# A hybrid DeltaNet and attention layer: the last stage in two phases with the output product as seven block products, and the attention merge moved beside the inverse and the scan

## The chip, the cores and the metric

One core of a Trainium2 chip runs the whole layer as one program. The metric is the time of one execution in device microseconds; the median of three runs is given. The engines are named as in the profile: PE is TensorE (PEld its weight loads), DVE VectorE, ACT ScalarE, POOL GpSimd, SP the engine that issues the DMA transfers. Each executes its own instructions in order; semaphores order them between engines.

## The reference

x has 2048 tokens of 1024 channels in float32. One input projection feeds two token mixers of four heads of 128 channels: a gated DeltaNet in chunks of 64, whose unit lower-triangular matrices are inverted, and a dilated window attention in three groups, whose outputs are merged by their softmax denominators. Cut to what matters here:

```python
tmat = lax.linalg.triangular_solve(eye + lower, eye, left_side=True, lower=True, unit_diagonal=True)
...
xs = tuple(jnp.moveaxis(a, 2, 0) for a in (q, k, u, w, a_intra, gc))
_, o = lax.scan(step, s0, xs)
...
alpha = jax.nn.softmax(jnp.stack(lses, axis=0), axis=0)
o_swa = jnp.sum(alpha[..., None] * jnp.stack(outs, axis=0), axis=0)
o_dn = rms_norm(o_dn, dn_norm_w) * jax.nn.silu(dn_z);  y_dn = o_dn @ w_branch_dn
o_swa = o_swa * jax.nn.silu(swa_z);  y_swa = o_swa @ w_branch_swa
merged = jax.nn.sigmoid(g_dn) * y_dn + jax.nn.sigmoid(g_swa) * y_swa
x = x + merged @ w_out
```

The two branch products are 2048 x 512 by 512 x 1024 each, the output product 2048 x 1024 by 1024 x 1024.

## The kernel before, in words

Every product is made in three passes: each operand is split into a high part (`split`: ACT rounds to fp32r, L87) and the rest (a subtraction on DVE or POOL, L88), and high by high, high by low and low by high are summed in PSUM.

The work comes in this order, as PE sees it: the input projection of the attention part with the attention itself beside it (to some 1000 us); the projections of the DeltaNet part, of z and of the gates (`cunits`, L720 to L722, 24 matmuls 128x512 for each chunk of 128 columns and 512 tokens; three PSUM tiles `mm`); from 1976 us the last stage. Beside the projections' matmuls runs a list of events: every six matmuls `hook` counts one tick, and what `at(delay, ...)` put down for that tick is issued there. Where a pool or the scheduler leaves an instruction free, its place on its engine may still differ from the place in the code.

Beside the projections run, in turn: the inverse of the 128 triangular matrices on DVE (`inverse`, 63 rows, each a product L1020 and a reduction L1023; M is stored to `vscr`, its transposed copy Z, made half by ACT in L1014 and half by DVE in L1015, to `tscr`); the scan over 16 tiles of 128 tokens (`scan`, its loads of `rec`, `t` from `tscr` and `vb` from `vscr` at L1042 to L1048, its first matmul L1058); in the last chunks, the tail, the loads and splits of the final weights (`w_fin`, `w_split`), and the first attention merges. The gate chunks end in a tanh on ACT (L1155) and a store to `gscr`; their weights are split by L87 and L88.

`combine(t)` (L1187 to L1207) merges the three attention groups of a tile of 128 tokens: it loads `oc` (3 groups, 4 heads, 128 channels and two statistics, 780 KB) and does a dozen operations on DVE and one exponential on ACT. `o_prep` transposes a tile of a branch on PE (L1221), gates it with z on DVE (L1222) and splits it.

The last stage goes through eight blocks of 256 tokens. `fin_y` makes, for each of eight groups of 128 output channels, both branch products (L1237 to L1239, 24 matmuls 128x256), gates them on DVE (L1241), adds them on POOL (L1243) and splits the sum (L1244, L1245) into mh and ml. `fin_out` then multiplies mh and ml by w_out, four times 24 matmuls 128x512 (L1254 to L1256), adds x on DVE (L1260) and stores the result. So the output product of a block follows its branches at once, and the merges, loads and weight splits of later blocks run beside it.

## Time and profile before

| | us |
|---|---|
| median of 3 runs | 2356.08 (2354.23 to 2360.46) |
| the profiled execution | 2357.82 |
| its span, first to last instruction | 2356.0 |
| its mean granted TensorE clock | 0.99 |

The page gives busy time by engine, a chain of work followed back from the last instruction, and groups of instructions with the idle time before them. A row of the timeline has the start in the span, the duration, the engine, the line, the operation and its tiles, and in brackets the idle time of the engine before it and what ended it. Matmuls overlap, so their spacing, not their duration, is what one costs.

### The profile page before, as it was taken

The numbers are of one execution on the slowest core, as the hardware profiler recorded it, in microseconds if no ns is written. First come the engines' busy times: TensorE is split into PE (matmuls) and PEld (weight loads), VectorE is DVE, ScalarE is ACT, GpSimd is POOL, SyncE is SP. The second block draws the span as 40 slices with busy tenths as digits, with TensorE's granted clock in tenths as the row PEclk, the third lists the DMA queues.
The fourth block names the chain that finished last, engine by engine and source line by source line (L and its number), as shares of the span: only waits on it lengthen the run. The fifth ranks groups of instructions, "written<-read, shape, count | busy, mean of one in ns | idle before, by whom it ended". The sixth has DMA issues, their size and how long they took to land.

```text
span 2356.0 us, 43344 instructions
## 1 busy us (share of the span) xinstructions
PE 2297.1 (97%) x15216; PEld 2086.2 (89%) x15216; DVE 1347.7 (57%) x2853; ACT 907.2 (39%) x2948; POOL 889.2 (38%) x1331
## 2 busy tenths in 40 slices
...
GB/s 296 325 277 323 272 283 292 269 161 239 251 265 236 246 273 261 259 148 101 130 110 132 127 103 113 72 76 69 212 207 208 193 120 175 161 179 150 148 139 77
DMA packets 525969, 452.23 MB, mean 192 GB/s; under 512 B 66168, under 2 KB 490424, under 8 KB 523320
## 3 DMA queue, kind: packets, MB, share of 16 engines
...
q14 instruction: 96, 0.79, 0.1%
...
## 4 chain that ended last, share of the span: by engine, by line
PE 66%; DMA 5%; DVE 3%; POOL 1%; ACT 1%; issue 1%; SPq 0%; DVEq 0%; POOLq 0%; ACTq 0%
PE mm L433 12%; PE mm L720 10%; PE mm L721 10%; PE mm L722 10%; PE mm L1254 2%; PE mm L1256 2%; PE mm L1255 2%; PE mm L1237 2%; PE mm L1239 2%; PE mm L1238 2%; DMA oscr<-ol 2%; DMA gcb<-gcscr 1%; PE tp L584 1%; PE po L626 1%; DMA raw<-in_w_out_dram 1%; PE tp L617 1%
## 5 line engine op out<-in xcount | busy, mean ns | idle before, releaser
L720 PE MATMUL mm<-hh,w 128*128 128x512 f32 x1152 | 463.3, 402 | 0.0
L722 PE MATMUL mm<-hh,w 128*128 128x512 f32 x1152 | 457.8, 397 | 0.0
L721 PE MATMUL mm<-hl,w 128*128 128x512 f32 x1152 | 456.9, 397 | 0.0
L433 PE MATMUL mm<-w,hh 128*128 128x256 f32 x1760 | 328.3, 286 | 0.0
L433 PEld LDWEIGHTS mm<-w,hh 128*128 128x128 f32 x1760 | 271.2, 190 | 0.0
L88 POOL TENSOR_TENSOR w<-raw,w 128x512 fp32r<-128x512 f32 x68 | 100.0, 1472 | 435.0 <-ACT w L87 434.8
L720 PEld LDWEIGHTS mm<-hh,w 128*128 128x128 f32 x1152 | 220.3, 191 | 45.9
L722 PEld LDWEIGHTS mm<-hh,w 128*128 128x128 f32 x1152 | 217.0, 188 | 46.9
L433 PE MATMUL mm<-hh 128*128 128x256 f32 x880 | 257.5, 293 | 0.0
L721 PEld LDWEIGHTS mm<-hl,w 128*128 128x128 f32 x1152 | 217.6, 189 | 42.4
L433 PE MATMUL mm<-hl,hh 128*128 128x256 f32 x880 | 249.8, 284 | 0.9 <-POOL hl L295 0.9
L433 PE MATMUL mm<-hh,hl 128*128 128x256 f32 x880 | 249.6, 284 | 0.0
L433 PE MATMUL mm<-w,hl 128*128 128x256 f32 x880 | 248.3, 282 | 0.0
L607 DVE CUSTOM_DVE_ANT_0 p<-sc,mask 128x128 f32<-128x128 f32 (+1 forms) x192 | 70.0, 365 | 213.8 <-PE sc L604 87.0
L433 PEld LDWEIGHTS mm<-hl,hh 128*128 128x128 f32 x880 | 169.4, 192 | 1.3 <-POOL hl L295 1.3
L433 PEld LDWEIGHTS mm<-hh 128*128 128x128 f32 x880 | 169.3, 192 | 0.0
L433 PEld LDWEIGHTS mm<-hh,hl 128*128 128x128 f32 x880 | 169.0, 192 | 0.0
L433 PEld LDWEIGHTS mm<-w,hl 128*128 128x128 f32 x880 | 166.1, 189 | 0.0
L368 POOL TENSOR_SCALAR st<-st 128x4 f32<-128x4 f32 x96 | 21.1, 219 | 374.0 <-ACT junk L367 371.9
L1237 PE MATMUL mm<-oh,hh 128*128 128x256 f32 x512 | 143.7, 281 | 1.7 <-DVE gt L1241 1.7
L1239 PE MATMUL mm<-oh,hl 128*128 128x256 f32 x512 | 142.9, 279 | 0.0
L1238 PE MATMUL mm<-ol,hh 128*128 128x256 f32 x512 | 142.9, 279 | 0.0
...
## 6 DMA issues: line engine op xcount, KB each, us to landing
...
qks<-rec SPq DMA_DIRECT2D x96, 256.0 KB, 3.2
raw<-in_w_in_dram SPq DMA_DIRECT2D x68, 256.0 KB, 3.3
gscr<-gt SPq DMA_DIRECT2D x64, 256.0 KB, 2.5
gt<-gscr SPq DMA_DIRECT2D x64, 256.0 KB, 3.4
...
```

What stands on the lines that cost most here:

```text
L88: eng.tensor_tensor(out=l, in0=raw, in1=h.bitcast(F32), op=ALU.subtract)
L433: mm = lambda x, y, **kw: nc.tensor.matmul(o, x, y, skip_group_check=True, **kw)
L607: nc.vector.tensor_tensor_reduce(out=p[:, lo:hi], in0=sc[:, lo:hi], in1=self.mask[:, slot * P + lo:slot * P + hi], scalar=3e38, scale=-SCA ...
L720: nc.tensor.matmul(pr, wh[:, k, :], a, start=(k == 0), stop=False)
L721: nc.tensor.matmul(pr, wh[:, k, :], b, start=False, stop=False)
L722: nc.tensor.matmul(pr, wl[:, k, :], a, start=False, stop=(k == KT - 1))
L1237: nc.tensor.matmul(o, self.wbh[:, k, ms], oh[:, k, :], start=(k == b * 4), stop=False)
L1238: nc.tensor.matmul(o, self.wbh[:, k, ms], ol[:, k, :], start=False, stop=False)
L1239: nc.tensor.matmul(o, self.wbl[:, k, ms], oh[:, k, :], start=False, stop=(k == b * 4 + 3))
L1254: nc.tensor.matmul(pr, mh[:, k, cs], self.woh[:, k, hs], start=(k == 0), stop=False)
L1255: nc.tensor.matmul(pr, mh[:, k, cs], self.wol[:, k, hs], start=False, stop=False)
L1256: nc.tensor.matmul(pr, ml[:, k, cs], self.woh[:, k, hs], start=False, stop=(k == KT - 1))
```

## The change

Four things are changed.

1. `inverse` makes both halves of the transposed copy on DVE (L1018 of the changed kernel).
2. `combine` no longer runs in the tail and the last stage. One tile is merged every 15 ticks from the start of the inverse on, sixteen in all: the minimum on DVE (L1253), the exponential and the weighting of the groups (twelve operations 128x128, L1266) on ACT, all else on POOL (L1254 to L1262, the additions L1270); the tile is parked in DRAM, in `osd` (L1272), and `o_load` fetches it for `o_prep`. Tiles `oc` have two buffers. While the inverse runs, ACT and POOL keep the order of the code (`manual_schedule`).
3. The last stage does all eight blocks' branch products first. The merged sum goes to DRAM, to `mscr`; w_branch is laid out by output channel; the operands for w_out (four quarters and sums of them, `wo_chunk`) are made in blocks 0, 2, 4 and 5, two of them parked in DRAM and fetched in block 7.
4. Then the output product is made in eight groups of 256 tokens, each as seven block products of half size (the scheme of Strassen and Winograd, `PROD`), twelve matmuls 128x512 each. `m_op` prepares operands of tokens four products ahead; the partial results are added up in PSUM, on DVE and on POOL. z's factors 0.5 become 0.25, and the output's factor goes.

The order of DVE at the end of the inverse, before (L1020, L1023: a row of the inverse; L1015 its half of the copy; L1061 and L1084: the scan):

```order
L1023 TENSOR_REDUCE M<-Z 128x62
L1022 MEMSET M 128x1
L1020 TENSOR_TENSOR Z<-M 128x3969
L1021 MEMSET M 128x64
L1023 TENSOR_REDUCE M<-Z 128x63
L1022 MEMSET M 128x1
L1015 COPY Z<-M 128x2048
L1061 TENSOR_TENSOR zs<-sc,nbr 64x256
```

and in the changed kernel, where these lines are L1023, L1026 and L1018, and L1253 is the minimum in `combine` for tiles 12, 13 and 14:

```order
L1026 TENSOR_REDUCE M<-Z 128x62
L1025 MEMSET M 128x1
L1253 TENSOR_REDUCE cs<-oc 128x4
L1023 TENSOR_TENSOR Z<-M 128x3969
L1253 TENSOR_REDUCE cs<-oc 128x4
L1024 MEMSET M 128x64
L1026 TENSOR_REDUCE M<-Z 128x63
L1025 MEMSET M 128x1
L1018 COPY Z<-M 128x2048 x2
L1253 TENSOR_REDUCE cs<-oc 128x4
L1064 TENSOR_TENSOR zs<-sc,nbr 64x256
L1087 SCALAR_TENSOR_TENSOR rr<-sc,ksn,rec 128x128 x4
```

Three reductions that read a loaded tile `oc` have come between the last rows of the inverse, its copies and the scan.

SP's order at the same place, before (the stores of the inverse, L1012 and L1016, among loads of weights and stores of gates):

```order
L1156 DMA gscr<-gt 128x512
L697 DMA raw<-in_w_in_dram 128x4x128
L1156 DMA gscr<-gt 128x512
L1012 DMA vscr<-M 128x4096
L1016 DMA tscr<-Z 128x4096
L1156 DMA gscr<-gt 128x512 x2
L697 DMA raw<-in_w_in_dram 128x4x128
L1042 DMA rec<-rec 128x4x256
L1043 DMA rec<-rec 128x4x384
L1044 DMA lo_20483<-rec 64x4x64
L1046 DMA t_20487<-tscr 64x4x64
```

and after (L1272 parks a merged tile, L1241 loads the three groups of one, L1015 and L1019 are the stores of the inverse):

```order
L1159 DMA gscr<-gt 128x512
L1272 DMA osd<-oc 512x1x128
L1241 DMA oc<-oscr 128x1560
L1015 DMA vscr<-M 128x4096
L1019 DMA tscr<-Z 128x4096
L1159 DMA gscr<-gt 128x512 x2
L700 DMA raw<-in_w_in_dram 128x4x128
L1045 DMA rec<-rec 128x4x256
L1046 DMA rec<-rec 128x4x384
L1047 DMA lo_20785<-rec 64x4x64
L1049 DMA t_20789<-tscr 64x4x64
```

The two stores of the inverse now stand behind the parking of tile 12 and the load of tile 14.

DVE's order in the tail, before (L1222 gates a transposed tile, L1194 to L1206 merge the groups):

```order
L1194 TENSOR_REDUCE cs<-oc 128x4
L1195 TENSOR_TENSOR cs<-cs,oc 128x12
L1197 TENSOR_TENSOR cs<-cs,oc 128x12
L1198 TENSOR_REDUCE cs<-cs 128x4
L1222 SCALAR_TENSOR_TENSOR z<-tp,z 128x512
L1199 RECIPROCAL cs<-cs 128x4
L1200 TENSOR_TENSOR cs<-cs 128x12
L1203 TENSOR_TENSOR oc<-oc,cs 128x4x128 x3
L1205 TENSOR_TENSOR osw<-oc 128x512
L1206 TENSOR_TENSOR osw<-osw,oc 128x512
L1222 SCALAR_TENSOR_TENSOR z<-tp,dnw,z 128x512
```

and after (L1304 gates, L91 splits the branch weights):

```order
L1168 TENSOR_SCALAR dnw<-dnw 128x1
L1304 SCALAR_TENSOR_TENSOR z<-tp,dnw,z 128x512
L1304 SCALAR_TENSOR_TENSOR z<-tp,z 128x512
L1304 SCALAR_TENSOR_TENSOR z<-tp,dnw,z 128x512
L1304 SCALAR_TENSOR_TENSOR z<-tp,z 128x512
L91 TENSOR_TENSOR hl<-raw,hh 128x512
```

Nothing of the merge is left there. On PE nothing changes up to the end of the scan; in the last stage the 96 output matmuls of a block (L1254 to L1256) are gone from between the branch products, and 84 (L1411) for each group follow behind all of them.

The diff, cut to its core:

```diff
-                nc.scalar.activation(zt[:, 0:32, :], M.rearrange("p c i -> p i c")[:, 0:32, :], AF.Copy)
-                V.tensor_copy(zt[:, 32:64, :], M.rearrange("p c i -> p i c")[:, 32:64, :])
+                for r in (slice(0, 32), slice(32, 64)):
+                    V.tensor_copy(zt[:, r, :], M.rearrange("p c i -> p i c")[:, r, :])
...
+        self.W = {n: tuple(a[:, s, 4 * h:4 * h + 4, :] for a in (self.hh, self.hl))
+                  for n, (s, h) in (("B11", (2, 0)), ("B21", (2, 1)), ("T3", (3, 0)), ("B22", (3, 1)),
+                                    ("T1", (0, 0)), ("T4", (0, 1)))}
...
+    def wo_chunk(self, c):
+        nc, V = self.nc, self.nc.vector
+        cs = slice(c * P, (c + 1) * P)
+        r = {}
+        for n in FN:
+            r[n] = self.rawp.tile([P, 4, P], F32, name="raw") if n[2] == "1" else self.fp.tile([P, 4, P], F32, name="raw2", bufs=3)
+            off = (int(n[1]) - 1) * 512 * D + (int(n[2]) - 1) * 512 + c * P
+            nc.sync.dma_start(r[n], dr(self.i["w_out"], off, [[D, P], [P * D, 4], [1, P]]))
...
+        def first():
+            put("B11", r["B11"], V)
+            put("B22", r["B22"], nc.gpsimd)
+
+        def second():
+            sub(r["B11"], r["B12"], r["B11"])
+            t2 = r["T2"] = self.fp.tile([P, 4, P], F32, name="raw2", bufs=3)
+            sub(t2, r["B22"], r["B11"])
+            sub(r["B12"], r["B22"], r["B12"])
+
+        def fourth():
+            put("B21", r["B21"], V)
+            put("T3", r["B12"], nc.gpsimd)
+
+        def fifth():
+            sub(r["B21"], r["B21"], r["T2"])
+            put("T2", r["T2"], V)
+        for d, fn in ((6, first), (8, second), (10, lambda: park("T1", r["B11"], V)), (12, fourth), (14, fifth),
+                      (16, lambda: park("T4", r["B21"], nc.gpsimd))):
+            self.at(d, fn)
...
+    def comb_load(self, t):
+        oc = self.oc = self.cb.tile([P, G, H, 130], F32, name="oc", bufs=2)
+        self.nc.sync.dma_start(oc.rearrange("p g h c -> p (g h c)"),
+                               dr(self.oscr, t * P * G * H * 130, [[G * H * 130, P], [1, G * H * 130]]))
...
     def combine(self, t):
+        nc, cb, V = self.nc, self.cb, self.nc.gpsimd
+        oc = self.oc
+        if t < 15:
+            self.comb_load(t + 1)
+        sm = cb.tile([P, 4, 12], F32, name="cs", bufs=2)
         nm, ls = oc[:, :, :, 128], oc[:, :, :, 129]
         mn, e, c, r = sm[:, 0, 0:4], sm[:, 1, :].rearrange("p (g h) -> p g h", h=H), \
             sm[:, 2, :].rearrange("p (g h) -> p g h", h=H), sm[:, 3, 0:4]
+        nc.vector.tensor_reduce(out=mn.unsqueeze(2), in_=nm.rearrange("p g h -> p h g"), axis=mybir.AxisListType.X, op=ALU.min)
         V.tensor_tensor(out=e, in0=mn.unsqueeze(1).to_broadcast([P, G, H]), in1=nm, op=ALU.subtract)
+
+        def share():
+            nc.scalar.activation(e, e, AF.Exp)
+            V.tensor_tensor(out=c, in0=e, in1=ls, op=ALU.mult)
+            V.tensor_tensor(out=r, in0=c[:, 0], in1=c[:, 1], op=ALU.add)
+            V.tensor_tensor(out=r, in0=r, in1=c[:, 2], op=ALU.add)
+            V.tensor_tensor(out=r, in0=r, in1=self.mone, op=ALU.pow)
+            V.tensor_tensor(out=c, in0=e, in1=r.unsqueeze(1).to_broadcast([P, G, H]), op=ALU.mult)
+
+        def weigh(g):
+            for h in range(H):
+                nc.scalar.activation(oc[:, g, h, 0:P], oc[:, g, h, 0:P], AF.Identity, scale=c[:, g, h:h + 1])
+
+        def add(g):
+            o = oc[:, 0, :, 0:P]
+            V.tensor_tensor(out=o, in0=o, in1=oc[:, g, :, 0:P], op=ALU.add)
+            if g == 2:
+                nc.sync.dma_start(dr(self.osd, t * P * 512, [[512, P], [P, H], [1, P]]), o)
+        self.at(1, share)
         for g in range(G):
+            self.at(3 + g, lambda g=g: weigh(g))
+        for g in (1, 2):
+            self.at(4 + g, lambda g=g: add(g))
+        if t < 15:
+            self.at(15, lambda: self.combine(t + 1))
...
+    def o_plan(self, nb, d):
+        self.z = getattr(self, "z", {})
+        for j, (t, b) in enumerate(((2 * nb, 0), (2 * nb, 1), (2 * nb + 1, 0), (2 * nb + 1, 1))):
+            self.at(max(1, d + 3 * j - 4), lambda t=t, b=b: self.z_load(t, b))
+            self.at(d + 3 * j, lambda t=t, b=b: self.o_prep(t, b))
+            if b and nb < 7:
+                self.at(d + 3 * j + 1, lambda t=t: self.o_load(t + 2))
...
+    def fin_y(self, nb, m):
+        nc = self.nc
+        self.g_load(8 * nb + m + 2)
+        gt = self.gt.pop(8 * nb + m)
         pr = self.ps.tile([P, 512], F32, name="mm", bufs=3)
         for b in range(2):
             o = pr[:, b * 256:(b + 1) * 256]
+            oh, ol = self.o_tiles(nb, b)
+            for k in range(4):
+                wh, wl = self.wbh[:, m, 4 * b + k, :], self.wbl[:, m, 4 * b + k, :]
+                nc.tensor.matmul(o, wh, oh[:, k, :], start=(k == 0), stop=False)
+                nc.tensor.matmul(o, wh, ol[:, k, :], start=False, stop=False)
+                nc.tensor.matmul(o, wl, oh[:, k, :], start=False, stop=(k == 3))
             self.hook()
         nc.vector.scalar_tensor_tensor(out=gt, in0=gt, scalar=1.0, in1=pr.rearrange("p (b c) -> p b c", c=256),
                                        op0=ALU.add, op1=ALU.mult)
         nc.gpsimd.tensor_tensor(out=gt[:, 0, :], in0=gt[:, 0, :], in1=gt[:, 1, :], op=ALU.add)
+        nc.sync.dma_start(dr(self.mscr, nb * P * 2048 + m * 256, [[2048, P], [1, 256]]), gt[:, 0, :])
...
+        self.split(part[name] if name in part else ss[name], *self.m_slot(q), V if name in part else nc.gpsimd)
+        if i == 0:
+            new("S1", part["A21"], part["A22"], ALU.add)
+            new("S2", ss["S1"], part["A11"], ALU.subtract)
+            if g:
+                self.m_load(g + 1)
+        elif i == 2:
+            new("S3", part["A11"], part["A21"], ALU.subtract)
+        elif i == 4:
+            new("S4", part["A12"], ss["S2"], ALU.subtract)
...
+        for i, (_, tgt, first, wn) in enumerate(PROD):
+            q = 7 * g + i
+            self.at(1, lambda q=q: self.m_op(q + 4))
+            if first:
+                acc[tgt] = self.ps.tile([P, 512], F32, name="mm", bufs=3)
+            pr = acc[tgt]
+            ah, al = self.m_slot(q)
+            wh, wl = self.W[wn]
+            for k in range(4):
+                mm = lambda x, y, **kw: nc.tensor.matmul(pr, x, y, **kw)
+                mm(ah[:, k, :], wh[:, k, :], start=first and k == 0, stop=False, skip_group_check=True)
+                mm(ah[:, k, :], wl[:, k, :], start=False, stop=False, skip_group_check=True)
+                mm(al[:, k, :], wh[:, k, :], start=False, stop=(k == 3), skip_group_check=True)
+                if k % 2:
+                    self.hook()
+            if i == 0:
+                keep("p1", pr)
+            elif i == 1:
+                keep("u2", pr, hold["p1"])
+                plus("u2", 0, 1)
+            elif i == 2:
+                result(0, 0, pr, xo.pop((0, 0)))
+            elif i == 3:
+                keep("u3", pr, hold["p1"])
+                plus("u3", 1, 1)
+                plus("p1", 1, 0)
+            elif i == 4:
+                result(1, 1, pr, hold["u3"])
+            elif i == 5:
+                result(1, 0, pr, hold["p1"])
+            else:
+                result(0, 1, pr, hold["u2"])
...
+            ipin.enter_context(tc.manual_schedule(engines={E.Activation, E.Pool}))
             dst.close()
+            self.comb_setup(pool(bst, "cb"))
             self.inverse(pool(ist, "ip", "right"), start_scan)
...
+            ipin.close()
             ist.close()
             self.scan(pool(qst, "qp", "right"), start_fin)
...
+            self.o_load(0)
+            self.o_load(1)
+            self.o_plan(0, 8)
...
+        for nb in range(8):
+            if nb < 7:
+                self.o_plan(nb + 1, 4)
+            if nb in (0, 2, 4, 5):
+                self.wo_chunk((0, 2, 4, 5).index(nb))
+            if nb == 6:
+                self.at(8, lambda: self.m_load(0))
             for m in range(8):
-                self.fin_y(nb, m, oh, ol, mh, ml)
-                take((3, 3, 3, 3, 2, 2, 0, 0)[m])
-            if nb + 1 < nbk:
-                oh, ol = self.o_start(nb + 1, xo, 0 if nb else 6)
-            for t in (2 * nb, 2 * nb + 1):
-                for half in range(2):
-                    take(8)
-                    self.fin_out(t, half, mh, ml)
-            self.flush()
+                self.fin_y(nb, m)
+                if nb == 7 and m in (1, 3):
+                    self.fetch("T1" if m == 1 else "T4")
+                if nb == 7 and m < 4:
+                    self.at(3, lambda m=m: self.m_op(m))
...
+        self.p2 = pool(p2st, "p2", "right")
+        self.m_load(1)
+        for g in range(8):
+            self.group(g)
```

208 lines of the change are left out of this document (112 added, 96 removed).

## The prediction

> **What bounds the kernel now.** First the head of the page, the busy line and the chain that ended last:
>
> ```profile
> span 2356.0 us, 43344 instructions
> PE 2297.1 (97%) x15216; PEld 2086.2 (89%) x15216; DVE 1347.7 (57%) x2853; ACT 907.2 (39%) x2948; POOL 889.2 (38%) x1331
> PE 66%; DMA 5%; DVE 3%; POOL 1%; ACT 1%; issue 1%; SPq 0%; DVEq 0%; POOLq 0%; ACTq 0%
> ```
>
> TensorE is the bound, so a matmul that goes is worth its full spacing, and an edit elsewhere is worth only what PE stands still for it. Next the busy time by stretch, one of 128x512 matmuls alone and one of 128x256 alone:
>
> ```profile
> 1440.00:1640.00 200.00, 200.00 (x867) 163.72 (x866) 193.61 (x243) 31.95 (x54) 31.54 (x18) 1.00 0.23 73
> 1976.00:1990.00 14.00, 14.00 (x120) 13.96 (x119) 8.56 (x12) 7.57 (x14) 6.73 (x7) 1.00 0.85 233
> ```
>
> The columns after the stretch and its length are PE, PEld, DVE, ACT and POOL busy with their counts, then the granted clock, the DMA share and GB/s. 200/867 = 0.2307 us for a 128x512 matmul, 14/120 = 0.1167 us for a 128x256 one. Last, what PE waited for in the second half of the run:
>
> ```profile
> PE tp L1221 <- DVE osw L1206: 3.9, 1, 3.9
> PE mm L1254 <- ACT mh L1244: 2.2, 3, 1.0
> PE mm L1237 <- DVE gt L1241: 1.7, 2, 1.4
> ```
>
> Little is to be had from waits, then: 8 us, and what follows them.
>
> **The matmuls.** Before, the last stage has 8 token blocks of 192 matmuls 128x256 and 96 of 128x512: 1536 x 0.1167 + 768 x 0.2307 = 356.4 us of the some 380 that the stage takes (1976 to 2356). After, the first phase has the same 1536, and the second 8 groups of 7 products of 12, that is 672 of 128x512. 96 are gone: 96 x 0.2307 = **-22.1 us**. Nothing else on PE changes in number; up to the end of the scan its order is the same.
>
> **The merge of the attention groups** leaves the tail of the projections. There the trace has its one long wait:
>
> ```profile
> 1877.05 0.17 DVE L1194 TENSOR_REDUCE cs<-oc 128x4 f32<-128x12 f32 x1 [3.39 <-DMA oc<-oscr]
> 1879.09 4.05 DVE L1203 TENSOR_TENSOR oc<-oc,cs 128x512 f32<-128x512 f32 x3
> 1880.30 0.40 PE L722 MATMUL mm<-hh,w 128*128 128x512 f32 x1
> 1884.62 1.09 PE L1221 MATMUL tp<-ident,osw 128*128 128x128 f32 x4 [3.91 <-DVE osw L1206]
> 1886.36 0.63 PE L722 MATMUL mm<-hh,w 128*128 128x512 f32 x1
> 1886.78 0.63 PE L720 MATMUL mm<-hh,w 128*128 128x512 f32 x1
> 1881.00:1889.00 8.00, 4.38 (x13) 3.64 (x14) 4.96 (x7) 2.15 (x4) 4.73 (x4) 0.62 0.84 256
> ```
>
> The load of the three groups' tile lands late, DVE merges for 7 us, and PE waits 3.9. Then the granted clock is 0.62 over 8 us, and matmuls come 0.42 apart instead of 0.23: a loss of 8 x 0.38 = 3.0. After the change only a load of the merged tile stands there, issued with that of the DeltaNet tile that PE takes first, and what is late next is that transpose's z tile; I expect no wait. **-7 us** (-4 if a z tile is late).
>
> **The first block of the last stage.** Its weights are still being split while it runs:
>
> ```profile
> 1990.00:2000.00 10.00, 8.29 (x66) 7.68 (x65) 5.31 (x8) 3.66 (x7) 5.38 (x6) 1.00 0.79 217
> 2000.00:2007.00 7.00, 6.13 (x31) 4.42 (x29) 0.86 (x2) 1.57 (x4) 4.87 (x6) 1.00 0.30 94
> 2007.00:2012.00 5.00, 3.51 (x8) 2.20 (x9) 1.28 (x2) 0.73 (x2) 2.20 (x3) 0.72 0.41 115
> ```
>
> PE is idle 1.7 + 0.9 + 1.5 = 4.1 us, and a clock of 0.72 over 5 us costs 1.4: 5.5. The waits on mh and gt above lie here. In the changed code a branch product is followed by the next branch product, not by an output product that needs it, and the output weights come block by block over phase one. **-6 us** (-3 if half of it returns).
>
> **The merge beside the inverse** is where I see a new wait. In the trace DVE works through the inverse without a gap, and this is its end, with what hangs on it:
>
> ```profile
> 1645.32 5.09 DVE L1020 TENSOR_TENSOR Z<-M 128x3969 f32<-128x3969 f32 x1
> 1650.52 4.23 DVE L1023 TENSOR_REDUCE M<-Z 128x63 f32<-128x3969 f32 x1
> 1654.81 2.02 DVE L1015 COPY Z<-M 128x2048 f32<-128x2048 f32 x1
> 1654.78 3.94 ACT L1014 ACTIVATE Z<-M 128x2048 f32<-128x2048 f32 x1 [1.37 <-DVE M L1022]
> 1658.74 0.32 SPq L1016 DMA_DIRECT2D tscr<-Z  x1
> 1663.90 0.60 ACT L1155 ACTIVATE gt<-mm 128x512 f32<-128x512 f32 x1 [4.70 <-issue]
> 1670.90 0.69 SPq L1046 DMA_DIRECT2D t<-tscr  x1
> 1685.94 0.68 PE L1058 MATMUL sc<-t,lo 64*64 64x64 f32 x8
> oc<-oscr SPq DMA_DIRECT2D x16, 780.0 KB, 5.7
> gscr<-gt SPq DMA_DIRECT2D x64, 256.0 KB, 2.5
> gt<-gscr SPq DMA_DIRECT2D x64, 256.0 KB, 3.4
> L1109 ACT ACTIVATE os<-qs 128x128 f32<-128x128 f32 x64 | 19.0, 297 | 39.2 <-DVE qs L1105 23.2 <-issue 16.1
> L1115 POOL TENSOR_TENSOR oss<-oss,mhalf 128x2 f32<-128x2 f32 x32 | 22.3, 698 | 2.7
> L1112 POOL TENSOR_TENSOR oss<-cq 128x2 f32<-128x2 f32 x32 | 6.3, 196 | 7.7 <-DVE os L1118 7.7
> L1226 POOL TENSOR_TENSOR ol<-z,oh 128x512 fp32r<-128x512 f32 x30 | 41.2, 1385 | 37.2 <-ACT oh L1225 37.0
> ```
>
> The inverse's result is stored, loaded again by about 1674.5 (1670.90 and the 3.4 us of the gt load), and PE needs it at 1685.9: 11 us of slack. Both copies on DVE are done at 1654.8 + 2 x 2.02 = 1658.9, where ACT's half was done at 1658.7: nothing. But DVE's order now holds a small reduction for each merged tile, at fixed places between the inverse's rows, and each waits for its tile's load; there are two such tiles, so the load of tile 12 waits until tile 11 has been parked.
>
> Followed by hand, with ACT's scaling at the price of L1109 (12 x 0.30 = 3.6), a small POOL operation 0.2 and the power 0.7, an addition 1.4: tile 11's reduction stands behind row 60 of the inverse, near 1629; POOL does the small operations of tiles 10 and 11 together (3.0) and a weight split (1.3), ACT the scaling, POOL two additions (2.8), which ends near 1641, 1643 if one meets a DVE operation; 2.5 for the store (as gscr's), 5.7 for the load of tile 12: 1649 to 1651. DVE stands at that reduction from 1645.2. From there the last row and the copies take 5.1 + 4.2 + 4.0 = 13.3, so the copies end near 1664 and not 1659. SP is next: the two stores of the inverse now stand behind the parking of tile 12 and the load of tile 14. Tile 12's chain from 1650 on is 2.1 + 3.6 + 2.8 + 2.5 = 11: the stores leave near 1662, and if each step meets a blocked engine, near 1672. ACT queues too: the gate chunks' tanh, 5.5 us apart, stand behind the scalings of tiles 12, 13 and 14, and when three chunks' PSUM tiles are taken PE stops. Tile 14 loads near 1663 + 5.7 = 1669, its reduction and small operations take 2.1 and half of its scalings 1.8: 1673, where PE, three PSUM tiles on, needs that chunk's tanh (1663.90 before) two chunks later, by about 1675. And POOL's clearing of the vb tiles waits behind tile 14. Early end: all fits in the slack, **0**. Late end: the stores leave at 1672 instead of 1659, 13 late with 11 of slack, and the tanh of the chunk beside tile 14 comes at 1684, 9 late, with the clock lowered behind it: **14**. I take **+8**, nearer to the late end's tanh than to nothing, since every step above is in a queue that stops in order.
>
> **A price that speaks against the change.** POOL's additions and DVE's two-input rows disturb each other in this trace; the first and the last of seven such rows, each between undisturbed ones:
>
> ```profile
> 1445.29 1.43 POOL L88 TENSOR_TENSOR w<-raw,w 128x512 fp32r<-128x512 f32 x1 [18.12 <-ACT w L87]
> 1445.99 0.94 DVE L1020 TENSOR_TENSOR Z<-M 128x196 f32<-128x196 f32 x1
> 1447.88 0.39 DVE L1020 TENSOR_TENSOR Z<-M 128x225 f32<-128x225 f32 x1
> 1644.97 1.29 POOL L88 TENSOR_TENSOR w<-raw,w 128x512 fp32r<-128x512 f32 x1 [17.85 <-ACT w L87]
> ```
>
> The row of 196 took 0.94 where the longer one of 225 took 0.39, and the last (5.09, above) some 0.8 too long. At 0.5 to 0.9 the seven make 5 us for the 18 POOL operations of this stretch (x18 in its row), 0.28 each. The change adds 28 additions, and 84 small operations of a sixth of the length: 28 x 0.28 + 84 x 0.05 = 12 us on DVE. Up to 6 of it only replaces the wait at tile 12.
>
> The Trainium skill, "SBUF — State Buffer", section "SBUF: two separate sides", says that DVE with two SBUF inputs and GpSimd take one shared port pair as an exclusive lock, and the loser blocks for the whole instruction. The trace agrees, with 0.94 against 0.39 us. By that rule at its worst, each addition in DVE's way, the sum would be that of the rival on the lock below.
>
> **Phase one's transfers.** A block moves 8 gate tiles, 4 z tiles and 4 attention tiles of 262 KB and stores 8 of 131 KB: 5.2 MB, and in the four blocks that build w_out operands another 8 x 262 KB, 7.3 MB. It has 192 x 0.1167 + transposes, 24 us: 218 and 306 GB/s, where the last stage before had 123 to 233. The trace's busiest stretch,
>
> ```profile
> 1876.00:1881.00 5.00, 4.70 (x23) 3.54 (x21) 3.48 (x9) 1.85 (x4) 1.49 (x2) 1.00 1.03 330
> ```
>
> gives 320 at full share, the first of the last stage 233/0.85 = 274. So a loaded block needs 22.9 to 26.8 us: -1 to +2.8 in each of four. Bounds 0 and 11; **+4**. DVE and POOL have room:
>
> ```profile
> L1241 DVE SCALAR_TENSOR_TENSOR gt<-gt,mm 128x512 f32<-128x512 f32 x64 | 43.8, 685 | 105.7 <-POOL ml L1245 51.4 <-PE mm L1239 38.3 <-DMA gt<-gscr 13.9
> L1243 POOL TENSOR_TENSOR gt<-gt 128x256 f32<-128x256 f32 x64 | 48.0, 750 | 139.6 <-DVE gt L1241 139.4
> ```
>
> 8 x 0.69 + 4 x 0.7 = 8.3 us of DVE and 8 x 0.75 + 4 x 1.39 = 11.6 of POOL in 24, and by like prices some 16 each in a loaded block.
>
> **The change of phase and phase two.** The second token block's merged tile can load only when phase one's buffers are closed; a megabyte costs between nothing (four products of 2.8 us cover it) and 10 us; **+2**. In a group, by the same prices, DVE has some 11 and POOL 10 of 19.4 us, and operands are made four products ahead; each eviction has one product, 2.8 us, for 0.7: 0. The last result is stored as before.
>
> **Sum.** The profiled execution took 2357.8 (span 2356.0), 1.7 above the median of the runs, 2356.1. 2357.8 - 22.1 - 7 - 6 + 8 + 4 + 2 = 2336.7, less 1.7: 2335.
>
> **Rivals.**
> - *No new wait*: the merge fits in the slack and the transfers in the blocks, 2335 - 12 = 2323. For it: 11 us of slack, DMA at 0.25 beside the inverse. Against: the in-order queues.
> - *Lock*: POOL's moved work prolongs the inverse by more than it has slack. At 12 us, with 6 of them replacing a wait, 2335 + 6 = 2341 (inside the forecast's range); if every addition blocks DVE for its whole 1.3 us and every small one for 0.2, 28 x 1.3 + 84 x 0.2 = 53 us, less 11 of slack and in place of my 8: 2335 + 34 = 2369, **slower**. It decides from a mean of about 1.0 us for each addition on. Against it: 0.28 measured.
> - *Transfers bound phase one*: 50 MB at the 233 GB/s of the last stage's first stretch take 216 us instead of 192: 2335 - 4 + 24 = 2355, the same; slower from below 220 GB/s. Against: 330 seen.
> - *The change doesn't do what it says*: each of the eight groups waits for its first operand, 2 us each with a lowered clock behind, and the 16 us eat the product saved: 2351.
>
> **How the numbers follow.** Forecast 0.50 (2322 to 2348 by its bounds: +6 and -12, and 7 for edits that return), no new wait 0.18, lock at its worst 0.08, transfers 0.12, groups 0.12. About 0.3%, 7 us, is what a measurement of this kernel tells from no change: faster means below 2349, slower above 2363. Forecast and no wait are faster but for 0.03; half of the groups' case and a quarter of transfers' are: 0.65 + 0.06 + 0.03 = 0.74. Same: 0.03 + 0.06 + 0.06 = 0.15. Slower: the lock's 0.08 and 0.03 of transfers, 0.11. The range leaves the slower cases out and takes the others: 2318 to 2359.
>
> **What would show it.** 672 matmuls of 128x512 in the last stage, 0.23 apart: the matmul term. No wait at the first transposes, clock 1.00 from 1876 to 1889: the merge's removal. DVE's idle time before the reductions of tiles 12 to 14, the time of the store of tscr, and any PE wait between 1660 and 1700: the new wait. The excess of the inverse's two-input rows over their neighbours: the lock. PE waits on gt or z in blocks 0, 2, 4 and 5: the transfers. The forecast is wrong if the inverse ends before 1659 or after 1672, or if phase one takes over 203 us.

## The result, and the profile after

| | before | after |
|---|---|---|
| median (range) of four runs, us | 2355.15 (2350.77 to 2360.46) | 2410.81 (2404.66 to 2413.96) |
| profiled execution, us | 2357.82 | 2413.96 |
| scan's first matmul, in its span | 1685.9 | 1700.3 |
| first branch product | 1976.2 | 1992.4 |
| first output product | 2001.3 | 2244.5 |
| last matmul | 2352.0 | 2408.0 |

The changed kernel is slower: ratio 1.0232, 95% interval 1.0202 to 1.0263. The forecast was a gain of 21 us; it is a loss of 56. The head of the page after, with the busy line and the chain that ended last, by engine and by line:

```profile
span 2412.2 us, 43902 instructions
PE 2298.8 (95%) x15120; PEld 2083.1 (86%) x15120; DVE 1353.8 (56%) x2786; ACT 978.5 (41%) x3151; POOL 1035.3 (43%) x1460
PE 6%; DMA 6%; POOL 1%; issue 1%; DVE 1%; SPq 0%; ACT 0%; DVEq 0%; POOLq 0%; ACTq 0%
PE mm L1411 6%; DMA mscr<-gt 4%; DMA gt<-gscr 2%; POOL gt L1340 1%; DMA raw<-in_w_out_dram 0%; POOL hl L91 0%; SPq L1322 0%; DVE gt L1338 0%; POOL w L1308 0%; DVE raw L1367 0%; PE mm L1335 0%; PE mm L1336 0%; PE mm L1334 0%; POOL ol L1308 0%; ACT hh L90 0%
```

There are 96 matmuls fewer, yet PE is busy as long as before (2297.1). One reason can be read below: phase one's matmuls keep PE busy for 212 us at a granted clock of 0.93, and for 192 at 1.00 in `e12_no_operands`. The chain is followed back for some 15% of the span only, but what it finds there is telling: beside the block products (L1411, phase two) stand the store of the merged sum (`mscr<-gt`, 4%, some 96 us) and the load of the gate tiles (`gt<-gscr`, 2%), no longer matmuls alone. By stretch (the columns of the prediction's windows): the tail, phase one, its end, phase two.

```profile
1880.00:1992.00 112.00, 112.00 (x495) 91.68 (x494) 16.95 (x25) 29.91 (x51) 19.61 (x17) 1.00 0.50 151
1992.00:2244.00 252.00, 212.44 (x1647) 207.58 (x1646) 90.52 (x124) 36.68 (x61) 108.95 (x106) 0.93 0.67 192
2244.00:2290.00 46.00, 40.81 (x164) 31.78 (x163) 27.82 (x31) 11.47 (x20) 24.09 (x17) 0.93 0.63 218
2290.00:2405.00 115.00, 115.00 (x503) 94.22 (x502) 50.36 (x66) 23.18 (x38) 47.16 (x37) 1.00 0.40 132
```

The tail is without a gap at full clock, and so is phase two after its start. Phase one took 252 us for matmuls worth 192: PE stood still for 40 of them, and the other 20 went with the lowered clock of 0.93. Transfers fill only 0.67 of it. What the engines waited for there, PE over the second half of the run and SP over phase one (engine and line, what it waited for, us in total, times, longest):

```profile
PE mm L1334 <- DVE gt L1338: 16.3, 10, 5.6
PE mm L723 <- ACT gt L1158: 10.1, 3, 5.0
PE mm L1334 <- ACT oh L1307: 8.0, 3, 3.5
PE mm L1335 <- POOL w L1308: 6.3, 4, 3.4
SPq L1322 <- DMA mscr<-gt: 103.4, 40, 4.2
SPq L1341 <- POOL gt L1340: 28.5, 19, 4.9
```

PE waits for the gating (L1338) to free a PSUM tile, and for operands of its next block (L1307, L1308: `o_prep`). Behind both stands SP: the load of a gate tile (L1322) waits 40 times, 103 us in all, for a store of `mscr` to land.

### The profile page after: what moved, and what is told of

The parts are those of the page before. It is cut to its first block, busy times and chain, and to the rows that moved or that the text cites. A ratio compares the mean times of both kernels' runs of the same rounds, so it can differ in the third digit from the quotient of the medians.

```text
span 2412.2 us, 43902 instructions
## 1 busy us (share of the span) xinstructions
PE 2298.8 (95%) x15120; PEld 2083.1 (86%) x15120; DVE 1353.8 (56%) x2786; ACT 978.5 (41%) x3151; POOL 1035.3 (43%) x1460
## 5 line engine op out<-in xcount | busy, mean ns | idle before, releaser
L723 PE MATMUL mm<-hh,w 128*128 128x512 f32 x1152 | 465.3, 404 | 10.1 <-ACT gt L1158 10.1
L91 POOL TENSOR_TENSOR w<-raw,w 128x512 fp32r<-128x512 f32 x68 | 96.9, 1429 | 240.8 <-ACT w L90 223.5
L837 DVE SCALAR_TENSOR_TENSOR acc<-xr,cw,acc 128x512 f32<-128x512 f32 x144 | 121.1, 841 | 17.1 <-ACT acc L835 11.5
L594 ACT ACTIVATE kq<-tp 128x256 fp32r<-128x256 f32 x148 | 56.3, 381 | 178.9 <-PE tp L587 177.9
L613 ACT ACTIVATE p<-p,ol 128x128 f32<-128x128 f32 (+1 forms) x192 | 88.1, 459 | 64.0 <-DVE ol L610 63.7
```

The source lines that it names most:

```text
L91: eng.tensor_tensor(out=l, in0=raw, in1=h.bitcast(F32), op=ALU.subtract)
L594: nc.scalar.activation(h, src, AF.Copy)
L613: self.at(1, lambda: nc.scalar.activation(p[:, lo:hi], p[:, lo:hi], AF.Exp, bias=ol[:, 128:129], scale=-1.0, accum_out=ol[:, 129:130]))
L723: nc.tensor.matmul(pr, wh[:, k, :], a, start=(k == 0), stop=False)
L837: nc.vector.scalar_tensor_tensor(out=acc, in0=xr[:, j:j + 512], scalar=w[:, j:j + 1], in1=acc, op0=ALU.mult, op1=ALU.add)
```

## Experiments

The first question is what made phase one 59 us longer than its matmuls, the second what moved its begin from 1976 to 1992. Each kernel has the changed one as its base; from `e2_sum_tile` on, all but `e3_pinned` and `e4_merge_left_out` have the edit of `e2_sum_tile` too. Times in us, in the span of the profiled execution:

| kernel | median, us | ratio to before (95%) | scan begins | phase one begins | its length |
|---|---|---|---|---|---|
| before | 2355.15 | 1 | 1685.9 | 1976.2 | - |
| after | 2410.81 | 1.0232 (1.0202 to 1.0263) | 1700.3 | 1992.4 | 252.2 |
| e1_other_tile | 2367.71, one run | | 1700.1 | 1988.9 | 211.9 |
| e2_sum_tile | 2377.27 | 1.0096 (1.0076 to 1.0117) | 1697.7 | 1988.0 | 221.1 |
| e12_no_operands | 2350.96, one run | | 1701.5 | 1991.7 | 193.0 |
| e7_parking | 2417.89 | 1.0265 (1.0247 to 1.0282) | 1748.0 | 2031.8 | 218.5 |
| e13_built_on_pool | 2405.83 | 1.0194 (1.0165 to 1.0222) | 1703.7 | 1995.0 | 243.0 |
| e4_merge_left_out | 2385.5, one run | | 1683.5 | 1967.4 | 251.4 |
| e3_pinned | 2430.54 | 1.0324 (1.0306 to 1.0343) | 1713.0 | 2012.5 | 251.6 |
| e6_small_on_dve | 2411.78 | 1.0235 (1.0214 to 1.0256) | 1709.4 | 2018.4 | 222.0 |
| e5_merge_in_scan | 2420.55 | 1.0280 (1.0262 to 1.0297) | 1743.5 | 2027.3 | 223.7 |
| e8_merge_after_inverse | 2397.37 | 1.0159 (1.0138 to 1.0181) | 1686.4 | 2007.8 | 223.8 |
| e9_both | 2395.12 | 1.0144 (1.0128 to 1.0161) | 1686.0 | 2008.7 | 218.7 |
| e10_split_merge | 2377.43 | 1.0075 (1.0058 to 1.0092) | 1686.2 | 1990.9 | 219.4 |
| e14_pool_and_spread | 2396.55 | 1.0165 (1.0135 to 1.0196) | 1688.2 | 1993.5 | 243.0 |
| e11_act_copy | 2383.8 | 1.0108 (1.0093 to 1.0123) | 1703.7 | 1995.5 | 220.0 |

The changed kernel, `e1_other_tile`, `e2_sum_tile`, `e12_no_operands` and `e13_built_on_pool` have the same merge and the same code up to the scan. Their scans begin between 1697.7 and 1703.7 and their phase one between 1988.0 and 1995.0, so a few us in these two columns tell nothing.

### Phase one: a round trip, or the rate of transfers?

The chain of waits of the changed kernel, in a piece of phase one (start, duration, step):

```profile
2085.94 4.68 DMA mscr<-gt
2090.68 0.36 SPq L1322
2091.09 4.98 DMA mscr<-gt
2096.09 0.38 SPq L1322
2096.57 4.52 DMA mscr<-gt
2101.11 3.38 DMA gt<-gscr
2104.69 0.70 DVE gt L1338
```

For three stores it goes through no engine that computes. Over the whole of phase one this store makes 36.2% of the chain, the load 17.4%. A store lands; only then does SP issue the load that goes into the same buffer (L1322); the next store, long ready, stands behind that load in SP's order, and so on: in this piece one tile every 5.3 us (2085.94, 2091.09, 2096.57), where PE makes the 24 matmuls for one in 2.8. Two experiments cut this loop: one stores constants from another tile and leaves the merged sum out of the output, one adds into a tile of its own (and makes the parked low part in place, for the room).

```diff
+        self.cst = op.tile([P, 256], F32, name="cst", bufs=1)
+        nc.vector.memset(self.cst, 0.01)
...
-        nc.sync.dma_start(dr(self.mscr, nb * P * 2048 + m * 256, [[2048, P], [1, 256]]), gt[:, 0, :])
+        nc.sync.dma_start(dr(self.mscr, nb * P * 2048 + m * 256, [[2048, P], [1, 256]]), self.cst)
```

> Phase one stores the same bytes to mscr, but from a tile of constants and not from the gate tile, so that a gate tile is free again after POOL's addition and SP's stores wait for nothing (the merged sum is left out of the output). Theory A, the gate tiles go round too slowly (load, gating, addition, store, one after the other, with four tiles and in SP's order): phase one falls from 252 us to 195 to 210 and the run to about 2360. Theory B, the transfers fill the DMA engines: the bytes are the same, phase one stays at 240 to 255 and the run above 2400. Theory C, POOL's additions come late behind its splits: little changes too, 235 to 255.

```diff
-            h, l = (self.lp.tile([P, 4, P], F32R, name=x, bufs=1) for x in ("th", "tl"))
-            self.split(raw, h, l, eng)
+            h = self.lp.tile([P, 4, P], F32R, name="th", bufs=1)
+            self.split(raw, h, raw.bitcast(F32R), eng)
...
-        nc.gpsimd.tensor_tensor(out=gt[:, 0, :], in0=gt[:, 0, :], in1=gt[:, 1, :], op=ALU.add)
+        ms = self.fp.tile([P, 256], F32, name="ms", bufs=3)
+        nc.gpsimd.tensor_tensor(out=ms, in0=gt[:, 0, :], in1=gt[:, 1, :], op=ALU.add)
```

> The full computation: POOL adds into a tile of its own (three of 1 KB, made room for by splitting two operands in place), so that the gate tile is free after the addition. Theory A: phase one 195 to 215 us instead of 252, the run 2360 to 2375, and PE's waits on the gating's result (16 us) and on the gated branch tiles (23 us), whose z loads stand behind the same queue, both fall by more than half. Theory B: phase one above 240, the run above 2400. Theory C: the waits on POOL's split and addition stay, 230 to 250.

The first doesn't test what it was made for. Nothing holds a store of constants back, and all 64 went out ahead of phase one (the two times are the first and the last start):

```profile
L1343 SPq DMA_DIRECT2D mscr<-cst x64: 320/451/1462, 1894.7 to 1941.0; - x64
```

Its phase one had 42.2 MB to move and not the changed kernel's 48.6, so its 211.9 us fit theory B as well as theory A. The second decides. Its phase one moves 49.2 MB, no less than before the edit, and takes 221.1 us instead of 252.2; SP's wait of 103 us is gone, and DVE waits for gate tiles for 4.4 us instead of 67.4. Phase one of `e2_sum_tile` by windows:

```profile
1988.00:2209.00 221.00, 204.59 (x1648) 201.96 (x1647) 93.82 (x125) 37.20 (x61) 107.93 (x106) 0.95 0.75 223
```

The rate rose with the speed, from 192 to 223 GB/s, so it was a result and not the limit. The 31 us are the price of the round trip, but for what the second edit gave: with the parking tile `tl` two waits for its store went too, 6.9 us on DVE and 3.6 on POOL, and this was not tested alone. For the 28 that are left, the next kernel leaves out what builds the operands for w_out (`wo_chunk`, its loads, differences, splits and parking, and `fetch`); the block products then read what lies in those tiles.

```diff
-            if nb in (0, 2, 4, 5):
-                self.wo_chunk((0, 2, 4, 5).index(nb))
...
-                if nb == 7 and m in (1, 3):
-                    self.fetch("T1" if m == 1 else "T4")
```

> e2 without the building of w_out operands in phase one (their loads, splits, differences, parking and fetching are left out; the block products read what lies in those tiles). Theory H'', what e2 leaves (221 us, some 20 above the matmuls, transposes and their spacing) comes from that building, as DVE's gating stands behind differences and splits that wait for w_out loads: phase one 198 to 206 us, the run 2353 to 2364. Rival B'', it is the transfers and waits of the base loop (gate, z and attention tiles): phase one 213 or more.

```profile
1992.00:2184.00 192.00, 192.00 (x1642) 192.00 (x1641) 68.33 (x98) 22.72 (x36) 92.01 (x97) 1.00 0.71 206
```

PE busy 192.00 of 192.00 at clock 1.00: phase one in 193.0 us, with no wait, while transfers run at 0.71 and 206 GB/s. So all that is left is the building of the operands, its transfers and its work on the engines together: 28 us. How does it cost that, when DVE is busy for 94 us of 221? Two of DVE's longest waits in phase one of `e2_sum_tile` stand before operations of the building, one for ACT's rounding and one for the loads of w_out:

```profile
DVE hl L91 <- ACT hh L90: 16.1, 4, 7.3
DVE raw L1205 <- DMA raw<-in_w_out_dram: 13.4, 4, 8.1
```

DVE's timeline shows what stands behind such a wait:

```profile
2002.49 0.68 DVE L1304 SCALAR_TENSOR_TENSOR z<-tp,z 128x512 f32<-128x512 f32 x1
2008.09 0.69 DVE L91 TENSOR_TENSOR raw<-raw,th 128x512 fp32r<-128x512 f32 x1 [4.92 <-ACT th L90]
2008.69 1.28 DVE L1338 SCALAR_TENSOR_TENSOR gt<-gt,mm 128x512 f32<-128x512 f32 x2
```

A subtraction for the parked operand waits 4.9 us for ACT; two gatings, with their PSUM tiles full, stand behind it and run back to back afterwards. Two kernels tried to take this away: a parking buffer with two halves and the building at other places, two ticks later, and all of the building on POOL.

```diff
+CH = ((0, 2), (1, 6), (3, 2), (4, 6))
...
+        pt = self.lp.tile([P, KT, 256], F32, name="mt", bufs=1).rearrange("p k c -> p (k c)").bitcast(F32R)
+        pk = {n: pt[:, j * 512:(j + 1) * 512].rearrange("p (k c) -> p k c", c=P) for j, n in enumerate(("T1", "T4"))}
...
-            h = self.lp.tile([P, 4, P], F32R, name="th", bufs=1)
+            h = pk[n]
...
-            if nb in (0, 2, 4, 5):
-                self.wo_chunk((0, 2, 4, 5).index(nb))
...
+                if (nb, m) in CH:
+                    self.wo_chunk(CH.index((nb, m)))
```

> e5 with the building of w_out operands spread evenly over blocks 0 to 5 and two ticks later behind its loads, and with a tile for each parked operand instead of one for both (five tiles for the merged sum). Theory H, what is left of phase one's loss after e2 (about 20 us above 200) is DVE's gating standing behind a weight split that waits for ACT's copy, which waits for the parking of the operand before: phase one falls from 221 to 202 to 212 us and the run 8 to 18 us below e5. Rival B', what is left is transfers: phase one stays within 4 us of 221.

```diff
         def sub(o, a, b):
-            V.tensor_tensor(out=o, in0=a, in1=b, op=ALU.subtract)
+            nc.gpsimd.tensor_tensor(out=o, in0=a, in1=b, op=ALU.subtract)
...
-            put("B11", r["B11"], V)
+            put("B11", r["B11"], nc.gpsimd)
...
-            put("B21", r["B21"], V)
+            put("B21", r["B21"], nc.gpsimd)
...
-            put("T2", r["T2"], V)
-        for d, fn in ((6, first), (8, second), (10, lambda: park("T1", r["B11"], V)), (12, fourth), (14, fifth),
+            put("T2", r["T2"], nc.gpsimd)
+        for d, fn in ((6, first), (8, second), (10, lambda: park("T1", r["B11"], nc.gpsimd)), (12, fourth), (14, fifth),
```

> e2 with all differences and low parts of the w_out operands on POOL, none on DVE: the same loads, stores and copies on ACT. Theory H-order, the 28 us between e2 (221) and e12 (193) arise because DVE's gating stands behind operations that wait for w_out loads and ACT's copies: phase one 196 to 207 us, the run 2355 to 2366. Rival H-transfers, the operands' 17 MB make the other loads late: phase one within 5 us of 221. Rival H-POOL, POOL becomes late with its additions: PE waits on gating that waits for gt loads, phase one 212 or more.

The first gave 218.5, where `e5_merge_in_scan`, the same kernel without it, has 223.7. That is some 5 us, and not the fall to between 202 and 212 that was forecast: the one buffer was not the main thing (the late begin of both has its cause in the merge, below). On POOL it came to 243.0, worse by 22. There PE waits for what stands behind the building on POOL's and ACT's queues instead:

```profile
PE mm L1334 <- ACT w L1307: 10.9, 3, 6.2
PE mm L1335 <- POOL w L1308: 7.3, 3, 3.5
PE mm L1335 <- POOL ol L1308: 4.5, 1, 4.5
```

This fits an account in which work that can wait holds up work that can't, on whichever engine it is put. It is argued from these waits and not shown: no kernel made here took the 28 us away, and what part of them is due to the transfers alone (four loads and four stores for each chunk, and the fetches; 49.2 MB in phase one against 39.6, where the expectation spoke of 17 MB) was not separated.

### The merge beside the inverse: what moved the begin by 16 us?

The merge's arithmetic is left out (only its first group is loaded and parked):

```diff
-        nc.vector.tensor_reduce(out=mn.unsqueeze(2), in_=nm.rearrange("p g h -> p h g"), axis=mybir.AxisListType.X, op=ALU.min)
...
-        self.at(1, share)
-        for g in range(G):
-            self.at(3 + g, lambda g=g: weigh(g))
-        for g in (1, 2):
-            self.at(4 + g, lambda g=g: add(g))
+        self.at(6, lambda: nc.sync.dma_start(dr(self.osd, t * P * 512, [[512, P], [P, H], [1, P]]), oc[:, 0, :, 0:P]))
```

> The merge's arithmetic beside the inverse and the scan is left out: a tile is loaded and its first group parked, with no work on DVE, ACT or POOL. This bounds what any order of that work could give: theories D and E alike expect PE's loss from 1430 to 1870 to fall from 70 to about 48 us (that of before, in the same reckoning), and the run to about 2390. If it falls less, the rest is the transfers' or the copies' on DVE.

Phase one begins at 1967.4 instead of 1992.4; 0.4 of that was there before the inverse, so the moved merge costs **24.6 us**, or 20.6 to 27.6 by the spread of the kernels with the same merge: 16.4 up to the scan's first matmul (1700.3 against 1683.5), 8.2 after it. From the scan's first matmul to phase one this kernel takes 283.9, before took 290.2: the merge's removal from the tail was worth 6.4. (Two more kernels with no merge there, `e5_merge_in_scan` and `e7_parking`, take 283.8.) PE itself waits 10.1 us in the stretch of the inverse, all for the tanh on ACT (L1158, above), and 2.1 at the scan's start for `t`; without the merge it waits for neither.

Where the 16.4 come from stands in the timelines of the changed kernel at the inverse's end, DVE's first:

```profile
1639.91 4.16 DVE L1023 TENSOR_TENSOR Z<-M 128x3844 f32<-128x3844 f32 x1
1644.18 4.10 DVE L1026 TENSOR_REDUCE M<-Z 128x62 f32<-128x3844 f32 x1
1657.05 0.18 DVE L1253 TENSOR_REDUCE cs<-oc 128x4 f32<-128x12 f32 x1 [8.76 <-DMA oc<-oscr]
1657.15 4.78 DVE L1023 TENSOR_TENSOR Z<-M 128x3969 f32<-128x3969 f32 x1
1664.61 0.17 DVE L1253 TENSOR_REDUCE cs<-oc 128x4 f32<-128x12 f32 x1 [2.68 <-DMA oc<-oscr]
1669.04 4.54 DVE L1018 COPY Z<-M 128x2048 f32<-128x2048 f32 x2
1678.09 0.17 DVE L1253 TENSOR_REDUCE cs<-oc 128x4 f32<-128x12 f32 x1 [4.52 <-DMA oc<-oscr]
1673.60 0.32 SPq L1019 DMA_DIRECT2D tscr<-Z  x1
```

The prediction's wait is there, at the reductions of tiles 12, 13 and 14: 8.8, 2.7 and 4.5 us, and the inverse is stored at 1673.6 instead of 1658.7. That the loads are late comes from the chain before them, POOL's small operations and ACT's scaling:

```profile
1631.85 3.99 POOL L1254 TENSOR_TENSOR cs<-cs,oc 128x12 f32<-128x12 f32 x1 [7.96 <-DVE cs L1253]
1639.98 4.16 POOL L1262 TENSOR_TENSOR cs<-cs 128x12 f32<-128x12 f32 x1
1657.74 4.27 POOL L1254 TENSOR_TENSOR cs<-cs,oc 128x12 f32<-128x12 f32 x1
1644.34 3.62 ACT L1266 ACTIVATE oc<-oc,cs 128x128 f32<-128x128 f32 x12 [8.25 <-POOL cs L1262]
L1254 POOL TENSOR_TENSOR cs<-cs,oc 128x12 f32<-128x12 f32 x14 | 14.7, 1049 | 8.0 <-DVE cs L1253 8.0
```

A subtraction of 128x12 that takes 0.2 us alone took 4.3. At 1657.74 it begins 0.6 us behind DVE's row of 3969 and ends with it (1657.74 + 4.27 = 1662.01; 1657.15 + 4.78 = 1661.93). The first at 1631.85 and L1262 at 1639.98 do the same with their rows: the one at 1639.91 ends at 1644.07, and ACT's scaling, which waited 8.25 us for L1262, starts at 1644.34. From there on the chain takes what it was to take:

```profile
1646.86 2.65 POOL L1270 TENSOR_TENSOR oc<-oc 128x512 f32<-128x512 f32 x2 [2.56 <-ACT oc L1266]
1649.54 0.53 SPq L1272 DMA_DIRECT2D osd<-oc  x1
1652.17 0.33 SPq L1241 DMA_DIRECT2D oc<-oscr  x1
```

That is tile 10, added up and parked; then tile 12 is loaded into its buffer, and DVE's reduction follows at 1657.05. Without the 7.7 us that the two stretched operations took too long it would have come near 1649.4. DVE's copies do the same as its rows: these two ran beside the two copies that begin at 1669.04.

```profile
1669.70 2.01 POOL L1258 TENSOR_TENSOR cs<-cs,oc 128x12 f32<-128x12 f32 x1
1671.79 1.85 POOL L1259 TENSOR_TENSOR cs<-cs 128x4 f32<-128x4 f32 x1
```

Do the late small operations alone decide? The first kernel below does the small operations on DVE (a reciprocal for the power); the second pins DVE's and SP's order too, so that no reduction is placed ahead of its turn.

```diff
-        V.tensor_tensor(out=e, in0=mn.unsqueeze(1).to_broadcast([P, G, H]), in1=nm, op=ALU.subtract)
+        nc.vector.tensor_tensor(out=e, in0=mn.unsqueeze(1).to_broadcast([P, G, H]), in1=nm, op=ALU.subtract)
...
-            V.tensor_tensor(out=r, in0=r, in1=self.mone, op=ALU.pow)
+            nc.vector.reciprocal(r, r)
```

> e2 with the merge beside the inverse, but its small operations (a dozen values a row) on DVE and the power replaced by a reciprocal there; ACT's weighting and POOL's additions stay. Theory F: five or six waits of POOL for a DVE row go from each tile's chain, DVE's waits for tiles 12 to 14 fall from 16 us to under 7, phase one begins 6 to 16 us earlier than in e2 (1988), the run takes 2361 to 2371. Rival G: ACT's and POOL's large operations are unchanged, so phase one begins within 4 us of 1988; and DVE, which now waits for ACT's exponential in each tile, may lose up to 10 us.

```diff
-            ipin.enter_context(tc.manual_schedule(engines={E.Activation, E.Pool}))
+            ipin.enter_context(tc.manual_schedule(engines={E.Activation, E.Pool, E.DVE, E.SP}))
```

> The changed kernel, with DVE and SP too kept in the order of the code while the inverse runs, so that tile 10's reduction is the last before the copies and tiles 11 to 15 come behind them. Theory D, PE's loss near the inverse's end comes from DVE and SP waiting for tiles 12 to 14 in the inverse: DVE's 16 us of waits fall under 4, the store of tscr goes from 1673.6 back to 1657 to 1663, and the run falls by 8 to 18 us to 2392 to 2403. Rival E, the lock between POOL and DVE or the sheer work on ACT and POOL: the inverse ends as late as before or the tanh is as late, and the run stays within 4 us of 2411.

Both were misses. With the small operations on DVE the scan begins at 1709.4, later still: DVE waits 31.2 us for loads of `oc`. The additions still meet its rows (2.17 us each, 1.57 in the changed kernel, 1.29 off the inverse), and ACT's scaling now waits 50.2 us for the small operations in DVE's order; which of the two decides was not separated. With the order pinned it begins at 1713.0, and the gating of z (L1152) now stands behind rows of the inverse:

```profile
PE mm L723 <- DVE gt L1152: 16.8, 8, 6.1
```

Three more kernels change when the merge runs. The first only moves its start behind that of the scan:

```diff
-            self.comb_setup(pool(bst, "cb"))
+            cbp = pool(bst, "cb")
+            hold_cb.append(cbp)
             self.inverse(pool(ist, "ip", "right"), start_scan)
...
             self.scan(pool(qst, "qp", "right"), start_fin)
+            self.at(3, lambda: self.comb_setup(hold_cb[0]))
```

> e2 with the merge of the sixteen tiles begun when the inverse is done, beside the scan and the tail, at the same pace. Theory F, the merge's chain beside the inverse is slow because POOL's small operations and additions must wait for the end of DVE's long two-input rows (128x12 operations of 4 us near the inverse's end), and through the loads of tiles DVE and SP then wait for it: off the inverse the small operations take 0.2 us and the power 1.0, the scan begins at 1684 to 1688 as before, phase one at 1967 to 1978, and the run takes 2355 to 2367. Rival G, it is the amount of ACT and POOL work, wherever it lies: the stalls return in the scan, phase one begins after 1984, and the run stays at 2373 or more.

It didn't test that. Free of the pinned stretch, the merge was placed ahead of it: all 192 scalings between 1000 and 1430 us,

```profile
L1266 ACT ACTIVATE oc<-oc,cs 128x128 f32<-128x128 f32 x192 | 64.6, 397 | 60.9 <-POOL cs L1262 58.6 <-DMA osd<-oc 2.3
```

and there PE fell 60 us behind `e4_merge_left_out`, which has no such work. `e7_parking` carries the same edit, hence its late begin. In the next kernel the power's operand is made by DVE out of the finished inverse, so that no merge can come before it; then that with the parking of `e7_parking`, its building of operands four ticks later still:

```diff
+                V.tensor_scalar(out=self.mone, in0=Z[:, 4092:4096], scalar1=0.0, scalar2=-1.0, op0=ALU.mult, op1=ALU.add)
                 nc.sync.dma_start(dr(self.tscr, 0, [[4096, P], [1, 4096]]), Z)
```

> What e5 was to be: e2 with the merge held behind the inverse. The -1 for the power is now made by DVE from the inverse's result, so that no tile but the first two can be weighted before; in e5 the merge had been placed ahead of the inverse, between 1000 and 1430. Theory F: scan from 1684 to 1690, phase one from 1964 to 1976 (e4, with no merge work: 1967), the run 2352 to 2364. Rival G, the amount of ACT and POOL work wherever it lies: phase one begins after 1982 and the run stays at 2370 or more.

> e8 with the w_out operands built as in e7, and six ticks later behind their loads instead of two. Theory H', what is left in phase one is DVE's gating behind weight operations that wait for late w_out loads: phase one 203 to 213 us (e2: 221, e7: 218.5), the run 2338 to 2354, at or under the kernel before. Rival B', the transfers: phase one 216 or more and the run within 6 us of e8.

The inverse is as before (scan at 1686.4), and POOL's small operation takes 0.2 us again, now that DVE's long rows are past (groups from 1690 to 2011):

```profile
L1255 POOL TENSOR_TENSOR cs<-cs,oc 128x12 f32<-128x12 f32 x14 | 3.0, 215 | 18.1 <-DVE cs L1254 15.1 <-DMA od<-odn 3.0
```

But sixteen tiles in the scan and the tail hold up the tanh there (PE waits 12.6 us for it), and phase one begins at 2007.8. The parking takes 5 us off phase one again (218.7 against 223.8, not the forecast 203 to 213), and nothing off its begin. Last, half and half: tiles 0 to 8 beside the inverse, 9 to 15 behind it, 8 ticks apart with the building of operands spread and two parking tiles, or 16 ticks apart with the building on POOL.

```diff
-            V.tensor_tensor(out=r, in0=r, in1=self.mone, op=ALU.pow)
+            V.tensor_tensor(out=r, in0=r, in1=(self.mone if t <= 8 else self.mone2), op=ALU.pow)
...
-        if t < 15:
-            self.at(15, lambda: self.combine(t + 1))
+        if t < 15 and t != 8:
+            self.at(15 if t < 8 else 8, lambda: self.combine(t + 1))
...
+            self.at(4, lambda: self.comb_load(9))
+            self.at(10, lambda: self.combine(9))
```

> e2 with tiles 0 to 8 merged beside the inverse as there, tiles 9 to 15 only behind its copies and spread over the scan at half the spacing in ticks, and with two tiles for the parked operands (three gate tiles instead of four) and the building of w_out operands spread over blocks 0 to 6. Theory F: the merge costs only where its chain is long (near the inverse's end, in e2) or where it is crowded (the tail, in e8); spread out it costs under 8 us: inverse without a loss, scan from 1684 to 1690, phase one from 1968 to 1982. Theory H': phase one 203 to 214 us. Together 2338 to 2362. Rival G: the merge's amount of ACT and POOL work stalls the scan: phase one begins after 1986, run above 2365.

> e13 with tiles 0 to 8 of the merge beside the inverse and 9 to 15 behind it at 16 ticks each (e10 had 8 ticks and lost 14 us in the scan, none in the inverse). Theory F with crowding: half the pace halves the scan's loss, phase one begins at 1974 to 1984 (e2 1988, e10 1991), and with H-order the run is 2340 to 2356, under the kernel before. Rival G: the loss per tile in the scan is the same at any pace, phase one begins at 1988 or later, the run within 4 us of e13.

The scan begins on time in both (1686.2 and 1688.2), but from there to phase one they take 304.7 and 305.3 us, against 283.9 without the merge and 292.1 in the changed kernel. Twice the pace or half of it makes no difference, so it is not how closely the tiles follow each other; what in the scan they hold up was not found. The interval of `e10_split_merge`, 1.0058 to 1.0092, overlaps that of `e2_sum_tile`, 1.0076 to 1.0117: no gain is shown.

The last one gives half of the transposed copy back to ACT:

```diff
-                for r in (slice(0, 32), slice(32, 64)):
-                    V.tensor_copy(zt[:, r, :], M.rearrange("p c i -> p i c")[:, r, :])
+                nc.scalar.activation(zt[:, 0:32, :], M.rearrange("p c i -> p i c")[:, 0:32, :], AF.Copy)
+                V.tensor_copy(zt[:, 32:64, :], M.rearrange("p c i -> p i c")[:, 32:64, :])
```

> e2 with the inverse's copy split between ACT and DVE again, as before the change. The prediction put this edit at nothing: within 3 us of e2 (2377). Rival: ACT's half (3.9 us) falls among the scalings and the tanh that are late there, and the run is 3 to 8 us slower than e2; or DVE's second copy holds POOL's small operations for 2 us and the run is 2 to 5 us faster.

Its median is 6.5 us above that of `e2_sum_tile` (2383.8 against 2377.27), but the kernel before, measured beside each, was 4.3 us slower too (2358.92 against 2354.65). The ratios, 1.0108 (1.0093 to 1.0123) and 1.0096 (1.0076 to 1.0117), can't be told apart, and its scan begins at 1703.7 like that of `e13_built_on_pool`, which has the copy of the change. So no effect of this part of the change is shown; that agrees with the prediction's "nothing" and doesn't rule out some us either way.

No kernel made here is faster than the one before by its interval. `e12_no_operands` (2350.96, one run) is the nearest to what the two phases would give if the operands cost nothing, and even it lies within the range of the runs of the kernel before (2350.8 to 2363.8).

## Why the prediction was wrong

By its own signs the forecast fails twice: the inverse's last store leaves at 1673.6, behind 1672, and phase one takes 252 us, over 203.

**The matmuls, right.** Phase two has 672 matmuls in 163.4 us (2244.5 to 2408.0): 155.0 by the prediction's 0.2307, and some 8 lost at its start.

**The tail, right.** 6.4 us by `e4_merge_left_out` against 7; the windows from 1880 on show no gap.

**The first block, right as far as it goes.** Those stalls went; without the building of operands phase one has none at all (193.0 us against 192).

**The merge beside the inverse: right mechanism, wrong size.** It was to cost 8 us, 14 at most; it cost 24.6. The step that failed is the price of the chain behind a reduction: "a small POOL operation 0.2 and the power 0.7". Alone they take 0.21 and 1.02 us; beside the inverse L1254 took 1.05 in the mean and up to 4.3. At tile 12 two such operations make the whole difference: DVE goes on at 1657.05 and not at "1649 to 1651". (The chain is that of tile 10, whose buffer tile 12 takes, and not of tile 11, as the prediction has it.) And 8.2 of the 24.6 us were lost behind the scan's begin, where the prediction had no term; no run shows by what. The rival on the lock asked what POOL's work does to DVE's rows and found little, rightly: the reduction of row 62 is done at 1648.3 instead of 1645.2. It didn't ask what DVE's rows do to POOL's operations. The row of 0.94 against 0.39 us that the prediction quoted has DVE as the loser, against a POOL operation of 1.43; with DVE the winner for 4 us at a time, each link of the merge's chain can lose up to that. `e6_small_on_dve` shows a limit of this: with the small operations off POOL nothing was gained, so that their price alone makes up the 24.6 us is not shown.

**Phase one's transfers: wrong mechanism.** They were to cost 4 us, 11 at most; they cost 59. The step that failed took them as so many bytes at such a rate, and the rival that spoke against it ("Transfers bound phase one", 24 us) did so too. Neither followed a buffer around. A gate tile is loaded (4.4 us to landing), gated, added, stored (4.1), and only then free; the loads and the stores stand in one queue, SP's; so the load for a tile that is not yet free stops the store that would free the next one. The medians of both transfers, from phase one's issues (size, us from issue to landing):

```profile
gt<-gscr SPq DMA_DIRECT2D x60, 256.0 KB, 4.4
mscr<-gt SPq DMA_DIRECT2D x62, 128.0 KB, 4.1
```

That one queue and one buffer serve both can be read from the diff. The price would still have misled: with the 2.5 us of `gscr<-gt`, the prediction's row for a store, and 0.4 for the issue of the load the loop makes some 2.9 us a tile, hardly more than PE's 2.8; with the 4.1 measured here it makes 4.5 (both are estimates from these rows; the phase's mean is 252.2 / 64 = 3.9). The Trainium skill, "DMA: Bandwidth & Descriptors", section "Anatomy of one DMA — SWDGE (gpsimd) path", says that a wait for a semaphore is made by the sequencer that issues the transfer and not by the DMA engines. The section is about transfers that GpSimd issues; the 103.4 us that SP waited agree with it for SP's. Of the 59 us, some 31 are this loop (`e2_sum_tile`) and 28 the building of operands (`e12_no_operands`). The prediction had counted the latter as busy time ("some 16 each in a loaded block", of 24), which was right and beside the point: DVE was idle for more than half of phase one (90.5 us busy of 252), and PE waited 16.3 us for its gating all the same. By which way the building costs its 28 us stays open between the waits shown above and its transfers.

**The change of phase** was put at 2 us and cost 8 (163.4 - 155.0; 5 to 8 in the other kernels), by waits of the first products for the gating and the held partial results, 5.1 us, and the clock behind them (0.93).

The terms again, the prediction's own where no run gives them (the first and the third): -22.1 - 6.4 - 6 + 24.6 + 59 + 8 = 57; the profiled executions differ by 2413.96 - 2357.82 = 56.1. Of the rivals none describes it. The range reached to 2359 since every bound was taken from busy times and rates.
